# Decoder block on one core: three seven-product pairs, lower halves by an adding DMA, a rearranged tail

## The chip, the cores and the metric

The kernel runs on one core of a Trainium2 chip. The metric is device time in microseconds. TensorE multiplies, VectorE, ScalarE and GpSimd do element work, SyncE issues most DMAs.

## The reference

One post-norm decoder layer on 256 tokens of width 2048, in float32. It projects x to queries, keys, values and two gates, runs two causal attentions (a block-gated one, which for 256 tokens is plain causal attention, and a differential one), mixes them through two branch matrices and an output matrix, and normalizes. What the change touches is the second half:

```python
h = _layer_norm(DEEPNORM_ALPHA * h + mix, ln1_g[l], ln1_b[l])
g, u = jnp.split(h @ w_ffn_in, 2, axis=-1)          # 2048 -> 2 x 5632
ffn = (jax.nn.silu(g) * u) @ w_ffn_out              # 5632 -> 2048
h = _layer_norm(DEEPNORM_ALPHA * h + ffn, ln2_g[l], ln2_b[l])
```

## The kernel before

**Split products.** Every float32 product is three matmuls (`mm3`, lines 91 to 93). A weight tile is split into an upper half that ScalarE casts to fp32r (`split`, line 71) and a lower half, the rest, that VectorE subtracts (line 72). The activations are split the same way. A matmul takes a 128x128 stationary and a moving tile of 128x512.

**Feed-forward blocks.** The 256 rows are two row blocks (m = 0, 1). The first feed-forward matrix is worked in 11 column blocks of 512 gate and 512 up columns. Block 0 is done by two plain products (`product`). Blocks 1 to 10 go through `pair_product(j)`: eight pairs of K tiles, each with one 1 MB load by SyncE into a `raw` buffer of three (`load_pair`, line 716), and four accumulators in PSUM (gate and up, for each row block). The accumulator pool holds four, so the next block's first matmul needs one of this block's to be emptied.

An ordinary pair makes two upper and two lower halves 128x1024 wide (`halves`) and needs eight `mm3`, 24 matmuls. At the places in `SEVEN`, now pairs 4 and 6 of blocks 1 to 9, the 2x2 product of row blocks and K tiles is done with seven products instead of eight, 21 matmuls. VectorE then makes four combinations of the weights in place (lines 756 to 759), and ScalarE and VectorE split these too, as `t2` and `t3`. The activations' combinations are made once (`row_forms`). Three of the products gather in four PSUM tiles p1, p5, p6, p7 over the block's pairs of this kind; after the last one VectorE joins them (lines 771 to 774) and adds the accumulators at the block's end (lines 777 to 780). Then follow sigmoid, two multiplications and 32x32 transposes (line 264) for each row block.

**Buffers and order.** Upper and lower halves rotate through eight buffers each (`wh`, `wl`). The order of the instructions on each engine is laid out by the framework's planner from program order and its own durations, and is then fixed. `later(n, fn)` puts work n steps (`tick`) ahead in program order; a pair has two steps. `move_blocks` (line 286) is put eight steps ahead: 16 transfers of 32 KB within the chip, on SyncE's queue, which turn the transposed block into rows for the next product.

**Second matrix and tail.** The 44 K tiles of the second matrix are streamed once, and all eight accumulators of 128x512 (two row blocks, four column blocks) are held in PSUM. The last four K tiles (`TAIL`) are kept back for row block 1, so that row block 0 is done earlier: its residual, statistics and normalization (`norm`) run beside row block 1's remaining matmuls. `norm` has a fast form, two VectorE operations per piece, and a slow form, one ScalarE and two GpSimd operations. Row block 1's last column block is done in two halves of 256 columns; then residual, statistics, `norm` and stores follow.

Of the kernel before, what the change touches and what calls it, by code (L numbers as in the profile page):

```python
# [44 lines left out]
def decoder_block(ctx, tc, xT, x, wz, lam_qk, subln, wa, wb, wo, g1, b1, b1T, wf, wfp, wfo, g2, b2,  # L45
# [9 lines left out]
    def bigt(shape, dt, name):  # L55
        return big.tile([P] + shape, dt, tag="big", name=name)
# [4 lines left out]
    def small(name, n=4):  # L61
        return sm.tile([P, n], F32, tag="sm%d" % n, name=name)
# [487 lines left out]
    def cols(j):  # L550
        return slice(j * N, (j + 1) * N)
# [1 line left out]
    def quarters(*slow):  # L553
        return [(j * N, (j + 1) * N, j in slow) for j in range(4)]


    def norm(m, g, b, name, sink, pieces):
        mv = small("mv_" + name, 2)
        nc.vector.bn_aggr(mv, stats[m].rearrange("p a b -> p (a b)")[:, :6 * nstats[m]])
        rs = small("rs_" + name, 2)  # L560
        rsqrt_of(rs[:, 0:1], mv[:, 1:2], 1.0, LN_EPS)
        nc.vector.scalar_tensor_tensor(rs[:, 1:2], mv[:, 0:1], -1.0, rs[:, 0:1], op0=ALU.mult, op1=ALU.mult)
        for j, (c0, c1, slow) in enumerate(pieces):
            c = slice(c0, c1)
            h = hres[m][:, c]
            if not slow:
                nc.vector.scalar_tensor_tensor(h, h, mv[:, 0:1], g[:, c], op0=ALU.subtract, op1=ALU.mult)
                nc.vector.scalar_tensor_tensor(h, h, rs[:, 0:1], b[:, c], op0=ALU.mult, op1=ALU.add)
            else:
                nc.scalar.activation(h, h, AF.Identity, bias=rs[:, 1:2], scale=rs[:, 0:1])  # L570
                nc.gpsimd.tensor_mul(h, h, g[:, c])
                nc.gpsimd.tensor_add(h, h, b[:, c])
            sink(m, j, c, h)

    b1t = const.tile([P, KD], F32, name="b1t")
    nc.sync.dma_start(b1t, b1T)
    hth = [None] * NM
# [111 lines left out]

    SEVEN = (4, 6)
    forms = []

    def row_forms():
        ns = len(SEVEN)
        full = bigt([NM, 2 * ns, P], F32, "hfull")
        fs = bigt([4, ns, P], F32, "forms")
        hl = bigt([2, 4, ns, P], F32R, "formshl")
        for m in range(NM):  # L700
            for n, i in enumerate(SEVEN):
                nc.vector.tensor_add(full[:, m, 2 * n:2 * n + 2, :], hth[m][:, 2 * i:2 * i + 2, :], htl[m][:, 2 * i:2 * i + 2, :])
# [5 lines left out]
        split(fs, hl[:, 0], hl[:, 1])  # L708
        forms.append(hl)

    def stat_s(f, n):
        return forms[0][:, 0, f - 1, n, :], forms[0][:, 1, f - 1, n, :]

    def load_pair(j, i):
        raw = wp.tile([P, 4, N], F32, tag="raw", name="raw_fp%d_%d" % (j, i), bufs=3)
# [68 lines left out]
    for j in range(NB_F):  # L784
        if j % 2 == 0:

            act.append(bigt([2, 4, NM, 4, 32], F32, "act%d" % (j // 2)))
        rt = None
        ts_ = []

        def silu(m, gate):
            t = scr("sl%d_%d" % (j, m))
            nc.scalar.activation(t, gate, AF.Sigmoid)
            nc.vector.tensor_mul(t, t, gate)
            return t
# [12 lines left out]
        later(8, lambda j=j, rt=rt: move_blocks(act[j // 2][:, j % 2].rearrange("p i m h c -> p i (m h c)"),  # L808
                                                rt.rearrange("p b m n -> p b (m n)")))
# [12 lines left out]
    def sink2(m, j, c, h):  # L822
        nc.sync.dma_start(out[m * P:(m + 1) * P, c], h)

    def ffn_mm(m, kt, j, w, ac=None, c=slice(0, N)):
        ah, al, pairs = w
# [7 lines left out]

    HEAD = 2
    ahead = []
    for kt in range(KF):
        pairs = list(weights(wfo[kt * P:(kt + 1) * P, :], "fo%d" % kt))
        ahl = sp.tile([P, 2, S], F32R, tag="s", name="ahl%d" % kt)
        ah, al = ahl[:, 0, :], ahl[:, 1, :]  # L840
        part = act[kt // 8][:, kt % 8 // 4, :, :, kt % 4, :].rearrange("p i m c -> p m i c")
# [17 lines left out]
                ffn_mm(1, kt, j, w)  # L859
        else:  # L860
            done.append((kt, w))
    for j in range(NB_D):
        residual(0, cols(j), oacc[0, j])
    norm(0, lng2, lnb2, "ln2_0", sink2, quarters(2, 3))
    H = N // 2
    last = hres[1][:, cols(NB_D - 1)]
    nc.vector.scalar_tensor_tensor(last, last, ALPHA, oacc[1, NB_D - 1], op0=ALU.mult, op1=ALU.add)
    for j in range(NB_D - 1):
        for kt, w in done:
            ffn_mm(1, kt, j, w)  # L870
        residual(1, cols(j), oacc[1, j])
    j = NB_D - 1
    for i in range(2):
        rest = acc("rest%d" % i)[:, :H]
        for kt, w in done:
            ffn_mm(1, kt, j, w, rest, slice(i * H, (i + 1) * H))
        residual(1, slice(j * N + i * H, j * N + (i + 1) * H), rest, 1.0)
    norm(1, lng2, lnb2, "ln2_1", sink2, [(0, 512, False), (512, 896, True), (896, 1408, False), (1408, 1792, False),
                                         (1792, 2048, False)])


def _tables(half):
# [56 lines left out]
```

## Time and profile before

| | |
|---|---|
| runs, median (lowest, highest) | 1393.11 us (1388.95, 1393.82) |
| profiled execution, its own time | 1389.86 us |
| its span | 1388.1 us |
| TensorE busy | 1366.9 us (98%) |
| VectorE busy | 922.8 us (66%) |
| ScalarE busy | 638.0 us (46%) |
| GpSimd busy | 57.6 us (4%) |

The stages are limited by different things, so the shares of the whole span say little of one stage. Matmuls are pipelined: one shows 0.39 us, but the next starts before it ends. A gap of TensorE shows in the start times of a block's first matmul.

### The profile page before, as it was taken

The numbers are of one execution on the slowest core, as the hardware profiler recorded it, in microseconds if no ns is written. First come the engines' busy times: TensorE is split into PE (matmuls) and PEld (weight loads), VectorE is DVE, ScalarE is ACT, GpSimd is POOL, SyncE is SP. The second block draws the span as 40 slices with busy tenths as digits, with TensorE's granted clock in tenths as the row PEclk, the third lists the DMA queues.
The fourth block names the chain that finished last, engine by engine and source line by source line (L and its number), as shares of the span: only waits on it lengthen the run. The fifth ranks groups of instructions, "written<-read, shape, count | busy, mean of one in ns | idle before, by whom it ended". The sixth has DMA issues, their size and how long they took to land.

```text
span 1388.1 us, 16263 instructions
## 1 busy us (share of the span) xinstructions
PE 1366.9 (98%) x6104; PEld 1125.6 (81%) x6104; DVE 922.8 (66%) x1163; ACT 638.0 (46%) x859; POOL 57.6 (4%) x62
## 2 busy tenths in 40 slices
PE   9999999999999999999999999999999999999996
PEld 6788888888888888888888888787787888888885
DVE  6666566766545454575969887898778765545546
ACT  5363434546444434444634544445444455444440
POOL 1001010100000000100000000000000000000003
PEclk9999999999999999999999999999999999999998
DMA  8574645554464649573553654646646586555541
GB/s 291 182 299 145 235 153 196 196 198 152 159 240 145 246 157 369 189 263 120 176 179 139 244 223 175 232 158 243 223 170 230 193 310 244 187 193 201 184 150 61
DMA packets 57151, 279.45 MB, mean 201 GB/s; under 512 B 10224, under 2 KB 22640, under 8 KB 25712
## 3 DMA queue, kind: packets, MB, share of 16 engines
q1 hardware_dynamic: 57072, 278.41, 55.4%
q8 instruction: 48, 0.79, 0.2%
q14 instruction: 31, 0.25, 0.1%
HBM read 264.74 MB, written 2.10 MB: 192 GB/s over the span
## 4 chain that ended last, share of the span: by engine, by line
PE 83%; DVE 6%; DMA 6%; ACT 2%; issue 1%; SPq 0%; POOL 0%; ACTq 0%; DVEq 0%; POOLq 0%
PE oacc L93 5%; PE oacc L91 5%; PE oacc L92 5%; DMA raw_fp<-in_wfp 4%; PE acc_fg L91 4%; PE acc_fu L91 3%; PE acc_fg L93 3%; PE acc_fg L92 3%; PE acc_fu L93 3%; PE acc_fu L92 3%; PE acc_gA L91 2%; PE acc_gA L92 2%; PE acc_gB L92 2%; PE acc_gB L91 2%; PE acc_gB L93 2%; PE acc_gA L93 2%
## 5 line engine op out<-in xcount | busy, mean ns | idle before, releaser
L72 DVE TENSOR_TENSOR wl_fo<-raw_fo,wh_fo 128x1024 fp32r<-128x1024 f32 x88 | 107.3, 1224 | 106.5 <-ACT wh_fo L71 101.3
L71 ACT CAST wh_fo<-raw_fo 128x1024 fp32r<-128x1024 f32 x88 | 92.4, 1055 | 123.7 <-PE oacc L93 110.8
L93 PE MATMUL oacc<-wh_fo,ahl 128*128 128x512 f32 x348 | 135.5, 389 | 0.0
L92 PE MATMUL oacc<-wl_fo,ahl 128*128 128x512 f32 x348 | 135.4, 389 | 0.0
L91 PE MATMUL oacc<-wh_fo,ahl 128*128 128x512 f32 x348 | 135.4, 389 | 0.0
L93 PEld LDWEIGHTS oacc<-wh_fo,ahl 128*128 128x128 f32 x348 | 65.3, 188 | 13.8 <-DVE ahl L72 0.3
L92 PEld LDWEIGHTS oacc<-wl_fo,ahl 128*128 128x128 f32 x348 | 65.3, 188 | 13.7
L91 PEld LDWEIGHTS oacc<-wh_fo,ahl 128*128 128x128 f32 x348 | 65.3, 188 | 13.5
L72 DVE TENSOR_TENSOR wl_gA<-raw_gA,wh_gA 128x1024 fp32r<-128x1024 f32 x32 | 38.8, 1220 | 35.9 <-ACT wh_gA L71 35.9
L72 DVE TENSOR_TENSOR wl_o<-raw_o,wh_o 128x1024 fp32r<-128x1024 f32 x32 | 39.5, 1235 | 33.9 <-ACT wh_o L71 33.9
L71 ACT CAST wh_gA<-raw_gA 128x1024 fp32r<-128x1024 f32 x32 | 33.6, 1054 | 53.7 <-PE acc_brB L93 20.0
L71 ACT CAST wh_o<-raw_o 128x1024 fp32r<-128x1024 f32 x32 | 33.7, 1054 | 48.4 <-PE acc_o L93 33.5
L72 DVE TENSOR_TENSOR wl_gB<-raw_gB,wh_gB 128x1024 fp32r<-128x1024 f32 x32 | 38.6, 1222 | 19.6 <-ACT wh_gB L71 19.0
L91 PE MATMUL acc_o<-wh_o,mth 128*128 128x512 f32 x128 | 50.4, 394 | 0.0
L91 PE MATMUL acc_gA<-wh_gA,xth 128*128 128x512 f32 x128 | 50.2, 392 | 0.0
L91 PE MATMUL acc_gB<-wh_gB,xth 128*128 128x512 f32 x128 | 50.1, 391 | 0.0
L93 PE MATMUL acc_o<-wh_o,mtl 128*128 128x512 f32 x128 | 49.9, 390 | 0.0
L92 PE MATMUL acc_o<-wl_o,mth 128*128 128x512 f32 x128 | 49.8, 389 | 0.0
L93 PE MATMUL acc_gB<-wh_gB,xtl 128*128 128x512 f32 x128 | 49.8, 389 | 0.0
L92 PE MATMUL acc_gA<-wl_gA,xth 128*128 128x512 f32 x128 | 49.8, 389 | 0.0
L92 PE MATMUL acc_gB<-wl_gB,xth 128*128 128x512 f32 x128 | 49.8, 389 | 0.0
L93 PE MATMUL acc_gA<-wh_gA,xtl 128*128 128x512 f32 x128 | 49.8, 389 | 0.0
(498 smaller groups left out, 3723.8 us busy)
## 6 DMA issues: line engine op xcount, KB each, us to landing
raw_fp<-in_wfp SPq DMA_DIRECT2D x80, 1024.0 KB, 5.2
raw_fo<-in_wfo SPq DMA_DIRECT2D x44, 1024.0 KB, 4.8
raw_gA<-in_wz SPq DMA_DIRECT2D x16, 1024.0 KB, 4.8
raw_gB<-in_wz SPq DMA_DIRECT2D x16, 1024.0 KB, 5.0
raw_o<-in_wo SPq DMA_DIRECT2D x16, 1024.0 KB, 5.0
raw_vA<-in_wz SPq DMA_DIRECT2D x8, 1024.0 KB, 5.1
raw_qB<-in_wz SPq DMA_DIRECT2D x8, 1024.0 KB, 7.0
raw_kB<-in_wz SPq DMA_DIRECT2D x8, 1024.0 KB, 5.0
```

The lines of the kernel that those rows point to most:

```text
L71: nc.scalar.copy(hi, src)
L72: (eng or nc.vector).tensor_sub(lo, src, hi)
L91: nc.tensor.matmul(ac, xh, wh, start=start, stop=False)
L92: nc.tensor.matmul(ac, xh, wl, start=False, stop=False)
L93: nc.tensor.matmul(ac, xl, wh, start=False, stop=stop)
```

## The change

`SEVEN` becomes (1, 3, 5): three pairs of 21 matmuls in blocks 1 to 9. `row_forms` makes the combinations for three pairs, in two large buffers as before and two scratch tiles more, and is placed three steps into the product before block 1. In the pairs 0, 6 and 7 of each block (block 10 too), the lower half of the two up tiles is made without VectorE: ScalarE writes the negated cast into `wl`, casts into `wh`, and a DMA issued by GpSimd adds the raw tile to `wl`.

In the tail six K tiles are kept back; the splits of the first two of them lie in large buffers. The second normalization is written out in a fixed order. ScalarE copies most of g and b into PSUM tiles that have come free, and VectorE's fast form reads them there. Of row block 1 VectorE does columns 0 to 1408 and GpSimd two pieces of 320; before, it was one piece of 384. Two stores are issued from ScalarE's queue.

```diff
-    SEVEN = (4, 6)
+    SEVEN = (1, 3, 5)
...
-        hl = bigt([2, 4, ns, P], F32R, "formshl")
+        hl = bigt([2, 4, 2, P], F32R, "formshl")
+        more = [[sp.tile([P, 4, P], F32R, tag="s", name="forms%d_%d" % (n, k)) for k in range(2)] for n in range(2, ns)]
...
+    BY_DMA = (0, 6, 7)
+
+    def halves_by_dma(src, name):
+        wh = wp.tile([P, 2, N], F32R, tag="wh", name="wh" + name)
+        wl = wp.tile([P, 2, N], F32R, tag="wl", name="wl" + name)
+        nc.scalar.activation(wl, src, AF.Copy, scale=-1.0)
+        nc.scalar.copy(wh, src)
+        nc.gpsimd.dma_start(wl.bitcast(F32), src, accum_op=ALU.add)
+        return [(wh[:, a, :], wl[:, a, :]) for a in range(2)]
...
-                b22, b12 = halves(raw[:, 2:4], nm + "u")
+                b22, b12 = (halves_by_dma if i in BY_DMA else halves)(raw[:, 2:4], nm + "u")
...
+            later(3, row_forms)
             ups = product(wf[1], KD, stat_h, "fu0")
-            later(6, row_forms)
...
-    TAIL = 4
+    TAIL = 6
...
+    def waiting(src, name):
+        raw = wp.tile([P, 2048], F32, tag="raw", name="raw_" + name, bufs=3)
+        nc.sync.dma_start(raw, src)
+        for i in range(2):
+            both = bigt([4, N], F32R, "%s_%d" % (name, i))
+            split(raw[:, i * 1024:(i + 1) * 1024].rearrange("p (a n) -> p a n", n=N), both[:, 0:2, :], both[:, 2:4, :])
+            yield both[:, 0:2, :], both[:, 2:4, :]
...
+        load = waiting if KF - TAIL <= kt < KF - 4 else weights
+        pairs = list(load(wfo[kt * P:(kt + 1) * P, :], "fo%d" % kt))
...
+    def slow(m, c0, c1):
+        h = hres[m][:, c0:c1]
+        nc.scalar.activation(h, h, AF.Identity, bias=rs[m][:, 1:2], scale=rs[m][:, 0:1])
+        nc.gpsimd.tensor_mul(h, h, lng2[:, c0:c1])
+        nc.gpsimd.tensor_add(h, h, lnb2[:, c0:c1])
+
+    def fast(m, c0, c1, g, b):
+        h = hres[m][:, c0:c1]
+        nc.vector.scalar_tensor_tensor(h, h, rs[m][:, 2:3], g, op0=ALU.subtract, op1=ALU.mult)
+        nc.vector.scalar_tensor_tensor(h, h, rs[m][:, 0:1], b, op0=ALU.mult, op1=ALU.add)
...
+    share = [(0, N), (N, 2 * N), (2 * N, 2 * N + 384)]
...
+        nc.scalar.copy(gb[k, i], src[:, c0:c1])
...
+    with tc.manual_schedule():
+        for j in range(NB_D):
+            residual(0, cols(j), oacc[0, j])
...
+        moments(1)
+        shift(1)
+        ends = [(1408, 1728), (1728, 2048)]
+        for c in ends:
+            slow(1, *c)
+        for i, c in enumerate(share):
+            fast(1, *c, gb["g", i], gb["b", i])
+            put(nc.sync, 1, *c)
+        for c in ends:
+            put(nc.scalar, 1, *c)
```

## Rows read from the trace of the kernel before

**Rows 1.** The page: busy time by engine; shares of the chain of waits.
```profile
PE 1366.9 (98%) x6104; PEld 1125.6 (81%) x6104; DVE 922.8 (66%) x1163; ACT 638.0 (46%) x859; POOL 57.6 (4%) x62
...
PE 83%; DVE 6%; DMA 6%; ACT 2%; issue 1%; SPq 0%; POOL 0%; ACTq 0%; DVEq 0%; POOLq 0%
```

**Rows 2.** Windows: blocks 1 to 3, blocks 5 to 9, after the last matmul.
```profile
core 0: us, PE busy (x) PEld busy (x) DVE busy (x) ACT busy (x) POOL busy (x), PEclk, DMA share, GB/s
704.69:831.17 126.48, 126.48 (x559) 104.73 (x558) 101.30 (x118) 58.96 (x66) 0.00 (x0) 1.00 0.55 199
874.42:1091.19 216.77, 213.32 (x930) 173.76 (x931) 180.65 (x211) 101.57 (x115) 0.00 (x0) 1.00 0.56 205
1375.10:1388.10 13.00, 0.00 (x0) 0.00 (x0) 9.11 (x16) 0.71 (x1) 4.96 (x5) 0.66 0.34 125
```

**Rows 3.** Waits of 690 to 1100: who waited, for whom; total, times, longest.
```profile
DVE wlfp_5g L72 <- ACT whfp_5g L71: 36.2, 9, 4.9
...
DVE wlfp_4t L72 <- ACT whfp_4t L71: 10.8, 9, 1.2
DVE wlfp_6t L72 <- ACT whfp_6t L71: 10.7, 9, 1.2
...
PE acc_fg L91 <- DVE p L777: 3.6, 4, 1.2
```

**Rows 4.** Timeline of VectorE, one turn: start, duration, operation, idle before.
```profile
880.75 1.18 DVE L72 TENSOR_TENSOR wlfp_2g<-raw_fp,whfp_2g 128x1024 fp32r<-128x1024 f32 x1
...
882.99 1.22 DVE L72 TENSOR_TENSOR wlfp_3g<-raw_fp,whfp_3g 128x1024 fp32r<-128x1024 f32 x1
...
885.26 1.22 DVE L72 TENSOR_TENSOR wlfp_4g<-raw_fp,whfp_4g 128x1024 fp32r<-128x1024 f32 x1
...
891.17 2.36 DVE L72 TENSOR_TENSOR wlfp_4t<-raw_fp,whfp_4t 128x1024 fp32r<-128x1024 f32 x2 [1.19 <-ACT whfp_4t L71]
897.16 1.22 DVE L72 TENSOR_TENSOR wlfp_5g<-raw_fp,whfp_5g 128x1024 fp32r<-128x1024 f32 x1 [3.63 <-ACT whfp_5g L71]
...
923.58 1.19 DVE L72 TENSOR_TENSOR wlfp_2g<-raw_fp,whfp_2g 128x1024 fp32r<-128x1024 f32 x1
```

**Rows 5.** Timeline of SyncE's queue, the same turn.
```profile
880.85 10.01 SPq L286 DMA_DIRECT2D act<-rt  x16
890.98 27.47 SPq L716 DMA_DIRECT2D raw_fp<-in_wfp  x8
923.69 11.10 SPq L286 DMA_DIRECT2D act<-rt  x16
```

**Rows 6.** DMA issues: count, KB of each, median us to landing.
```profile
raw_fp<-in_wfp SPq DMA_DIRECT2D x80, 1024.0 KB, 5.2
...
act<-rt SPq DMA_DIRECT2D x176, 32.0 KB, 1.8
...
raw_qA<-in_wz SPq DMA_DIRECT2D x7, 512.0 KB, 5.6
```

**Rows 7.** Timeline of the tail, VectorE and GpSimd.
```profile
1367.51 0.26 DVE L559 BATCH_NORM_AGGREGATE mv_ln<-stats 128x2 f32<-128x24 f32 x1
...
1368.71 0.16 DVE L562 SCALAR_TENSOR_TENSOR rs_ln<-mv_ln,rs_ln 128x1 f32<-128x1 f32 x1 [0.39 <-POOL rs_ln L234]
...
1374.84 0.67 DVE L546 SCALAR_TENSOR_TENSOR hres<-hres,oacc 128x512 f32<-128x512 f32 x1
...
1376.93 0.40 DVE L546 SCALAR_TENSOR_TENSOR hres<-hres,rest 128x256 f32<-128x256 f32 x1
...
1377.83 0.29 DVE L559 BATCH_NORM_AGGREGATE mv_ln<-stats 128x2 f32<-128x30 f32 x1
...
1384.09 1.00 DVE L568 SCALAR_TENSOR_TENSOR hres<-hres,rs_ln,ln2b 128x384 f32<-128x384 f32 x2
...
1374.83 1.27 POOL L572 TENSOR_TENSOR hres<-hres,ln2b 128x512 f32<-128x512 f32 x1
...
1380.61 1.35 POOL L571 TENSOR_TENSOR hres<-hres,ln2g 128x384 f32<-128x384 f32 x1 [1.01 <-ACT hres L570]
```

More of the change, by code (lines that the diff above doesn't have):

```diff
@@ L554, in quarters @@
         return [(j * N, (j + 1) * N, j in slow) for j in range(4)]
[L557 to L573, printed above, removed]
     b1t = const.tile([P, KD], F32, name="b1t")
@@ L707, in row_forms @@
         nc.vector.tensor_sub(fs[:, 3], a[0][1], fs[:, 1])
-        split(fs, hl[:, 0], hl[:, 1])
-        forms.append(hl)
+        split(fs[:, :, 0:2], hl[:, 0], hl[:, 1])
+        for n in range(2):
+            forms.append([hl[:, k, :, n] for k in range(2)])
+        for n, hi_lo in enumerate(more):
+            split(fs[:, :, 2 + n], *hi_lo)
+            forms.append(hi_lo)
     def stat_s(f, n):
-        return forms[0][:, 0, f - 1, n, :], forms[0][:, 1, f - 1, n, :]
+        return tuple(t[:, f - 1, :] for t in forms[n])
     def load_pair(j, i):
@@ L818, in decoder_block @@
         oacc[0, j] = acc("oacc0_%d" % j)
-    TAIL = 4
+    TAIL = 6
     done = []
-    def sink2(m, j, c, h):
-        nc.sync.dma_start(out[m * P:(m + 1) * P, c], h)
     def ffn_mm(m, kt, j, w, ac=None, c=slice(0, N)):
@@ L836, in decoder_block @@
     ahead = []
+    def waiting(src, name):
[5 more added lines that the diff above has]
+            yield both[:, 0:2, :], both[:, 2:4, :]
     for kt in range(KF):
-        pairs = list(weights(wfo[kt * P:(kt + 1) * P, :], "fo%d" % kt))
+        load = waiting if KF - TAIL <= kt < KF - 4 else weights
+        pairs = list(load(wfo[kt * P:(kt + 1) * P, :], "fo%d" % kt))
         ahl = sp.tile([P, 2, S], F32R, tag="s", name="ahl%d" % kt)
@@ L861, in decoder_block, with moments @@
             done.append((kt, w))
-    for j in range(NB_D):
-        residual(0, cols(j), oacc[0, j])
-    norm(0, lng2, lnb2, "ln2_0", sink2, quarters(2, 3))
     H = N // 2
-    last = hres[1][:, cols(NB_D - 1)]
-    nc.vector.scalar_tensor_tensor(last, last, ALPHA, oacc[1, NB_D - 1], op0=ALU.mult, op1=ALU.add)
-    for j in range(NB_D - 1):
+    rs = [small("rs_ln2_%d" % m) for m in range(NM)]
+    def moments(m):
+        nc.vector.bn_aggr(rs[m][:, 2:4], stats[m].rearrange("p a b -> p (a b)")[:, :6 * nstats[m]])
+        rsqrt_of(rs[m][:, 0:1], rs[m][:, 3:4], 1.0, LN_EPS)
@@ new lines, in shift, with put @@
+    def shift(m):
+        nc.vector.scalar_tensor_tensor(rs[m][:, 1:2], rs[m][:, 2:3], -1.0, rs[m][:, 0:1], op0=ALU.mult, op1=ALU.mult)
+    def put(eng, m, c0, c1):
+        eng.dma_start(out[m * P:(m + 1) * P, c0:c1], hres[m][:, c0:c1])
+    def slow(m, c0, c1):
[7 more added lines that the diff above has]
+        nc.vector.scalar_tensor_tensor(h, h, rs[m][:, 0:1], b, op0=ALU.mult, op1=ALU.add)
@@ L869, in decoder_block, with copy, tail_mms @@
+    share = [(0, N), (N, 2 * N), (2 * N, 2 * N + 384)]
+    gb = {}
+    def copy(t, src, k, i):
+        c0, c1 = share[i]
+        gb[k, i] = t[:, :c1 - c0]
+        nc.scalar.copy(gb[k, i], src[:, c0:c1])
+    def tail_mms(j):
         for kt, w in done:
             ffn_mm(1, kt, j, w)
[L871 to L877, printed above, removed]
@@ L878, in decoder_block @@
-    norm(1, lng2, lnb2, "ln2_1", sink2, [(0, 512, False), (512, 896, True), (896, 1408, False), (1408, 1792, False),
-                                         (1792, 2048, False)])
+    with tc.manual_schedule():
+        for j in range(NB_D):
+            residual(0, cols(j), oacc[0, j])
+        last = hres[1][:, cols(NB_D - 1)]
+        nc.vector.scalar_tensor_tensor(last, last, ALPHA, oacc[1, NB_D - 1], op0=ALU.mult, op1=ALU.add)
+        moments(0)
+        copy(acc("g2_0"), lng2, "g", 0)
+        copy(acc("b2_0"), lnb2, "b", 0)
+        copy(tmp("g2_1"), lng2, "g", 1)
+        tail_mms(0)
+        shift(0)
+        slow(0, 2 * N, 3 * N)
+        slow(0, 3 * N, 4 * N)
+        for i in range(2):
+            fast(0, i * N, (i + 1) * N, gb["g", 0] if i == 0 else gb["g", 1],
+                 gb["b", 0] if i == 0 else lnb2[:, N:2 * N])
+            put(nc.sync, 0, i * N, (i + 1) * N)
+        residual(1, cols(0), oacc[1, 0])
+        copy(tmp("b2_1"), lnb2, "b", 1)
+        tail_mms(1)
+        residual(1, cols(1), oacc[1, 1])
+        copy(tmp("g2_2"), lng2, "g", 2)
+        for i in range(2, NB_D):
+            put(nc.sync, 0, i * N, (i + 1) * N)
+        tail_mms(2)
+        residual(1, cols(2), oacc[1, 2])
+        copy(tmp("b2_2"), lnb2, "b", 2)
+        j = NB_D - 1
+        for i in range(2):
+            rest = acc("rest%d" % i)[:, :H]
+            for kt, w in done:
+                ffn_mm(1, kt, j, w, rest, slice(i * H, (i + 1) * H))
+            residual(1, slice(j * N + i * H, j * N + (i + 1) * H), rest, 1.0)
+        moments(1)
[8 more added lines that the diff above has]
+            put(nc.scalar, 1, *c)
```

## Prediction

> **What bounds the kernel now.** I read the busy times and the chain of waits first, then the stretch of the feed-forward blocks in windows, the waits in it, one block's turn on VectorE and on SyncE's queue, and at last the tail. TensorE is busy for 98% of the span and holds 83% of the chain [rows 1]; a matmul count taken off it is time taken off, as long as its operands arrive. In the ten paired blocks (j = 1 to 10) they arrive only just. Blocks 1 to 3 take 126.48 us, 42.16 each [rows 2]. By the code each has six ordinary pairs of 24 matmuls and two of 21, 186 together, so a matmul costs 42.16 / 186 = 0.2267 us and nothing is lost there. Blocks 5 to 9 take 216.77, 43.35 each [rows 2], with the same 186: they lose 1.2 us apiece. The reader is to see where: the first matmul of a block waits for the VectorE addition that empties its accumulator (L777), 3.6 us in four visible waits [rows 3], so VectorE arrives late at the end of a block.
>
> VectorE is not late for lack of rate: it is busy 180.65 of 216.77 us, 36.1 a block [rows 2]. It is late because its queue is in order and has three gaps a block: 4.0 us before pair 5 (36.2 over nine), 1.2 before the second half of pair 4 and 1.2 before that of pair 6 (10.8 and 10.7 over nine) [rows 3]. The two short ones are ScalarE's cast, which can begin only when the last of four in-place subtractions is done. The long one goes back to SyncE: its queue issues 16 small transfers in 10.01 us from 880.85 and the weight loads of pairs 5 and 6 stand behind them; they go out from 890.98 [rows 5], take about 5.2 us to land [rows 6], and VectorE starts pair 5 at 897.16 after 3.63 us of nothing [rows 4]. One turn, from pair 2 to the next block's pair 2, is 880.75 to 923.58, 42.83 us [rows 4], against 42.16 of TensorE. So the late blocks are VectorE's turn, and TensorE waits for it.
>
> **The matmuls removed.** One more pair of 21 in nine blocks: 27 matmuls, 6.1 us. TensorE's own block becomes 183 x 0.2267 = 41.48, so nine blocks need 373.3 where they take 1091.19 - 704.69 = 386.5 now. That is the ceiling, -13.2 us, if no operand is ever late. The last block, j = 10, has no such pair and stays.
>
> **What the third pair costs VectorE.** An ordinary pair occupies it from 880.75 to 882.99, 2.24 us. A seven-product pair starts at 885.26; its last double split starts at 891.17 and ends at 893.53: 8.27 us, 1.19 of it waiting [rows 4]. Turning one into the other adds 6.03. ScalarE gets two casts more, 1.8 us at its mean of 0.88 (101.57 / 115); it is idle for half of the block [rows 2], which covers them.
>
> **What the adding DMA gives back.** Three lower halves leave VectorE in each block. Half an ordinary pair is 1.12 us, so 3.4. ScalarE does one more cast for each, 2.6 us a block by the same mean; behind them stand the casts of pairs 7, 0 and 1 on its queue, which its idle half covers too. Thirty DMAs are issued by GpSimd, idle in this stretch. No row shows an adding DMA. The nearest from below is a 32 KB transfer inside the chip, 1.8 us; from above a load of equal size, 512 KB, 5.6 us [rows 6]. I take 4, nearer the equal size. It replaces a VectorE split of 1.22, so these halves come about 3 us later after their cast, and the raw buffer (one of three) is held as much longer before the next load may start. Pair 6's upper half needs it first: TensorE has six matmuls, 1.4 us, between the pair's start and the need. With loads behind it as late as now, this eats the lead and no more; at 5.6 it can stop TensorE by up to 2 us a block. By the Trainium skill, page DMA: Bandwidth & Descriptors, section Anatomy of one DMA, a transfer from GpSimd's queue costs about 2.0 us plus its bytes at 436 GB/s; the estimate from that is 3.2 us for 512 KB. It would make the lateness 2 us instead of 3 and leave the sum as it is.
>
> **The places.** With the three pairs at i = 1, 3, 5, the four additions that join the products (L771 to L774) run before pair 6, no longer in the last pair. That clears L777, the addition for which TensorE waits now. But pair 1's 8.27 us move into the same stretch.
>
> **The new turn.** Between the small transfers and pair 5 lie pairs 2, 3 and 4: two ordinary and one of seven products, before and after alike. So pair 5's load is as late as now, and its gap stays. Nothing in the change touches the 16 transfers or their place behind pair 4's load. The turn then is 43.35 + 6.03 - 3.4 = 46.0 us. If the order laid out by the planner fills one of the three cast gaps (it does put a split of pair 1 between the joining additions now, but fills neither cast gap), it is 44.8; I take that. It exceeds 41.48, so VectorE sets the block. At the start there is some lead (three blocks lost nothing), now used up in the first block: 41.5 + 8 x 44.8 = 399.9, against 386.5: **+13.4 us**. From below, with all gaps covered, it is -13.2; from above, with 46.0 from block 2 on, 41.5 + 368 = 409.5, +23.
>
> **The operand forms** are made some ten pair steps earlier, in the product before block 1, and are half as many again: three operations more on VectorE, wider ones besides, about 3 us at its mean of 0.86 (180.65 / 211) [rows 2], and a cast on ScalarE. The lead that let blocks 1 to 3 lose nothing covers them; without it, it is 3 us, once. Behind them on VectorE stand the lower halves of that product and of block 1's first pairs. Two more scratch tiles stay occupied; the six that are left are what one block uses.
>
> **The tail.** Now TensorE ends at 1375.10 and 13.00 us follow [rows 2]. VectorE reaches the last residual only at 1376.93 [rows 7], 1.8 us after its operand, because the first row block's normalization is still in its queue. Six K tiles kept back give 24 more matmuls, 5.4 us, to cover it, so the residual starts some 0.1 after TensorE. Then: residual to aggregate 0.9 (1376.93 to 1377.83); aggregate to the shift 1.2, as for the first row block (1367.51 to 1368.71), because no two-operand work of VectorE runs beside GpSimd's two small steps; 1.0 through the shift and ScalarE's first columns to GpSimd (1.01 idle now, for 384 columns); four GpSimd steps of 320. Such a step is between 1.27 x 320/512 = 0.8, the one beside a VectorE operation with its operand in PSUM, and 1.35 x 320/384 = 1.1 [rows 7]: 3.2 to 4.5. Last, 3.0 from the last result to the end (1385.09 to 1388.10). Sum 9.4 to 10.7; VectorE's side is 0.1 + 0.9 + 1.2 + 0.2 + 3.8 + 3.0 = 9.2, with 0.67 for 512 columns beside GpSimd [rows 7]. I take 10.0: **-3.0 us**. The six copies of g and b are ScalarE's, idle there; on the queue of ScalarE only the two last stores stand behind its work. The two K tiles in large buffers cost what the others cost; twelve more narrow matmuls add 0.1.
>
> The Trainium skill, page SBUF — State Buffer, section Who interferes with whom, says that a VectorE instruction with two SBUF inputs contends with a GpSimd instruction that reads SBUF, and the second to start blocks. Taken fully, a PSUM operand frees GpSimd and the steps are 0.8, a tail of 9.4; the trace's fastest step agrees, and the sum would move by 0.6.
>
> **Sum.** On the profiled execution of 1389.86 (span 1388.1, 1.8 around it): + 13.4 - 3.0 = 1400.3. The median of the runs, 1393.11, is 3.3 above that execution and their lowest, 1388.95, 0.9 below; halfway to the median gives **1402**. The likeliest case's own range is 1395 to 1411.
>
> **Rivals.**
> - *VectorE's gaps close* (the other side). The planner lays out the order anew, and a gap lasts only if nothing ready is queued in it. If pair 5's load gets ahead of the small transfers, or other work fills the 4.0 us, the turn is 42.0 and the nine blocks 41.5 + 8 x 42.0 = 377.5; with the cast gaps filled too, 373.3. With the tail: 1378 to 1374, some 1377 to 1381 as a median. It decides at a turn of 43.0. For it: L771 to L774 come earlier and VectorE's work without gaps, 37.0 (43.35 less 6.4 of gaps) + 4.8 - 3.4 = 38.4, is below 41.48. Against: those gaps were there in all nine blocks. Chance 0.36.
> - *It evens out*: half the long gap goes and a turn is 43.4: 41.5 + 347.2 = 388.7, +2.2 - 3.0, so 1389 to 1393. Chance 0.16.
> - *The adding DMA is the bound*: if it takes longer than a load of its size, both TensorE's wait for pair 6 and the next block's load after it grow, 3 us a block more: 1425. For it: three raw buffers, DMA engines busy 0.56 of the time already [rows 2]. Against: GpSimd is free, and the reads stay on the chip. Chance 0.10.
> - The forecast has 0.38.
>
> 0.5% is about what a measurement of this kernel can tell from no change, 7 us. Faster is the first rival, 0.36; same the second, 0.16; slower the rest, 0.48. The range 1375 to 1416 leaves out most of the third rival and the lower edge of the first.
>
> **What would show it.** Right: blocks 2 to 9 of 44 to 46 us, VectorE idle before pair 5 for about 4 us behind SyncE's 16 transfers, TensorE waiting inside seven-product pairs instead of at the block's first matmul, the tail near 10 us. Wrong: blocks of 41.5 (gaps closed), or TensorE's waits ending on the adding DMA.

## The result, and the profile after

The changed kernel takes **1442.45 us** (median of four, 1441.62 to 1443.09) where the kernel before, beside it, takes 1392.34: a ratio of 1.0365, 95% interval 1.0347 to 1.0382. It is slower by 50 us. The sign of the forecast holds; its size, 1402, and its range, up to 1416, do not.

The busy times of the page, which answer to [rows 1]: TensorE shows 21 matmuls fewer and more busy time, a first sign that matmuls ran slower or stood in line. (Line numbers are each kernel's own: in the changed kernel the in-place steps are L753 to L756, the joins L768 to L771 and the additions at a block's end L774 to L777.)
```profile
PE 1389.5 (96%) x6083; PEld 1125.5 (78%) x6083; DVE 928.3 (64%) x1188; ACT 681.8 (47%) x915; POOL 83.6 (6%) x94
```
Windows of the changed kernel, cut at the first matmul of a block: block 1, blocks 2 to 5, block 6, blocks 7 to 9, and what follows the last matmul. The columns are those of [rows 2].
```profile
704.37:750.29 45.92, 43.40 (x184) 35.42 (x183) 29.76 (x37) 21.44 (x24) 2.58 (x3) 0.96 0.67 209
750.29:947.38 197.09, 179.43 (x733) 138.28 (x732) 148.78 (x181) 99.36 (x114) 10.42 (x12) 0.97 0.67 210
947.38:994.35 46.97, 43.68 (x185) 33.65 (x183) 37.48 (x46) 22.97 (x27) 2.61 (x3) 1.00 0.64 206
994.35:1141.77 147.42, 135.54 (x550) 104.67 (x549) 112.31 (x136) 74.35 (x85) 7.83 (x9) 0.97 0.71 225
1431.12:1441.30 10.18, 0.00 (x0) 0.00 (x0) 5.25 (x10) 1.20 (x2) 4.14 (x6) 0.62 0.27 103
```
Nine blocks take 1141.77 - 704.37 = 437.4 us, 48.6 each, where they took 386.5 [rows 2]: +50.9. From block 10's first matmul to the last one it is 289.35 for 283.91 before, +5.4: pair 0's addition stops TensorE for 2.0 us there too, and the first products of the second matrix wait 1.1. The tail is 10.18 us for 13.00. With 0.3 us gained ahead of block 1 that makes the 53.2 us between the two profiled spans (1441.3 and 1388.1). GpSimd, the fifth busy time, now has three instructions a block: the issues of the adding DMAs. The granted clock is 0.96 to 0.97 in most blocks and 1.00 in block 6, which is also the second shortest.

The waits of the changed kernel from 690 to 1150 (who waited, for whom; total, times, longest), which answer to [rows 3]:
```profile
DVE p L774 <- PE acc_fg L93: 37.8, 8, 6.0
...
PE acc_fu L92 <- DMA wlfp_6u<-raw_fp: 18.4, 9, 2.7
...
PE acc_fu L92 <- DMA wlfp_0u<-raw_fp: 8.1, 7, 2.9
...
PE p L91 <- ACT whfp_1t L71: 6.8, 13, 1.2
```
TensorE stops at the adding DMA of pair 6 in all nine blocks and at that of pair 0 in most. And VectorE, which the forecast had as the bound, now waits for TensorE, 37.8 us: its addition of the first product (L774) cannot begin before the stopped matmuls are done.

The DMA issues of the changed kernel (count, KB of each, median us to landing), for [rows 6]:
```profile
wlfp_0u<-raw_fp POOLq DMA_DIRECT2D x10, 512.0 KB, 9.9
wlfp_6u<-raw_fp POOLq DMA_DIRECT2D x10, 512.0 KB, 5.3
wlfp_7u<-raw_fp POOLq DMA_DIRECT2D x10, 512.0 KB, 4.9
```
One stop, in the timelines of ScalarE, GpSimd and TensorE (start, duration, operation, idle before):
```profile
927.28 2.00 ACT L71 CAST whfp_5t<-raw_fp 128x1024 fp32r<-128x1024 f32 x2 [5.10 <-DVE raw_fp L756]
...
930.61 1.04 ACT L719 CAST whfp_6u<-raw_fp 128x1024 fp32r<-128x1024 f32 x1
931.55 1.06 ACT L718 ACTIVATE wlfp_6u<-raw_fp 128x1024 fp32r<-128x1024 f32 x1
```
```profile
932.91 0.87 POOL L720 DMA_DIRECT2D wlfp_6u<-raw_fp  x1 [41.51 <-ACT wlfp_6u L718]
```
```profile
935.97 0.39 PE L93 MATMUL acc_fg<-whfp_7g,htl 128*128 128x512 f32 x1
939.02 0.80 PE L92 MATMUL acc_fu<-wlfp_6u,hth 128*128 128x512 f32 x1 [2.65 <-DMA wlfp_6u<-raw_fp]
939.61 0.63 PE L93 MATMUL acc_fu<-whfp_6u,htl 128*128 128x512 f32 x1
...
942.13 0.40 PE L91 MATMUL acc_fu<-whfp_6u,hth 128*128 128x512 f32 x1
```
ScalarE works through its queue in order. It sits idle for 5.10 us until VectorE has done pair 5's in-place subtractions, casts pair 5's t halves, and only then pair 6. The addition is asked for at 932.91, TensorE is there at 936.36 (935.97 + 0.39) although the planner has already drawn matmuls of pairs 6 and 7 ahead, and the sum lands at 939.0: 6.1 us to landing against a lead of 3.4. After the stop the matmuls follow each other at about 0.43 us instead of 0.2267, seven steps in 3.11 us for 1.59: another 1.5 us. The clock in windows of 2 us goes with it: it falls to 0.50, the 1.2 GHz level, after the stop.
```profile
934.00:936.00 2.00, 2.00 (x10) 1.31 (x8) 1.58 (x2) 1.45 (x2) 0.25 (x1) 1.00 1.02 295
936.00:938.00 2.00, 0.37 (x2) 0.00 (x0) 0.25 (x1) 1.33 (x2) 0.62 (x1) 1.00 1.08 213
...
940.00:942.00 2.00, 2.00 (x6) 1.57 (x5) 0.00 (x0) 0.00 (x0) 0.79 (x1) 0.50 0.99 260
942.00:944.00 2.00, 2.00 (x10) 1.60 (x10) 0.28 (x1) 0.00 (x0) 0.00 (x0) 0.98 0.99 311
```

### The profile page after: what moved, and what is told of

It reads as the page before. It is cut to its first block, busy times and chain, and to the rows that moved or that the text cites. A ratio compares the mean times of both kernels' runs of the same rounds, so it can differ in the third digit from the quotient of the medians.

```text
span 1441.3 us, 16463 instructions
## 1 busy us (share of the span) xinstructions
PE 1389.5 (96%) x6083; PEld 1125.5 (78%) x6083; DVE 928.3 (64%) x1188; ACT 681.8 (47%) x915; POOL 83.6 (6%) x94
## 5 line engine op out<-in xcount | busy, mean ns | idle before, releaser
L72 DVE TENSOR_TENSOR wl_fo<-raw_fo,wh_fo 128x1024 fp32r<-128x1024 f32 x84 | 102.1, 1224 | 99.7 <-ACT wh_fo L71 95.1
L71 ACT CAST wh_fo<-raw_fo 128x1024 fp32r<-128x1024 f32 x84 | 87.7, 1054 | 115.3 <-PE oacc L93 95.0
L91 PE MATMUL oacc<-wh_fo,ahl 128*128 128x512 f32 x332 | 129.6, 390 | 1.2 <-DVE sl L791 0.9
L92 PE MATMUL oacc<-wl_fo,ahl 128*128 128x512 f32 x332 | 129.2, 389 | 0.0
L93 PE MATMUL oacc<-wh_fo,ahl 128*128 128x512 f32 x332 | 128.7, 389 | 0.0
L91 PEld LDWEIGHTS oacc<-wh_fo,ahl 128*128 128x128 f32 x332 | 62.3, 188 | 15.6 <-ACT ahl L71 1.3
L93 PEld LDWEIGHTS oacc<-wh_fo,ahl 128*128 128x128 f32 x332 | 62.3, 188 | 13.1
L92 PEld LDWEIGHTS oacc<-wl_fo,ahl 128*128 128x128 f32 x332 | 62.3, 188 | 12.6
L91 PE MATMUL acc_gB<-wh_gB,xth 128*128 128x512 f32 x128 | 50.1, 391 | 0.0
```

The lines of the kernel that those rows point to most:

```text
L71: nc.scalar.copy(hi, src)
L72: (eng or nc.vector).tensor_sub(lo, src, hi)
L91: nc.tensor.matmul(ac, xh, wh, start=start, stop=False)
L92: nc.tensor.matmul(ac, xh, wl, start=False, stop=False)
L93: nc.tensor.matmul(ac, xl, wh, start=False, stop=stop)
```

## Experiments

"Theory L" below is that an adding DMA costs what its landing overruns the lead that its cast has on TensorE; "theory H" that it costs by itself, by traffic and by the raw buffer that it holds. Each kernel was timed beside the kernel before (1389.9 to 1390.8 us). Pairs are counted from 0; three of the expectations below count them from 1 and say 1, 7 and 8 for the pairs 0, 6 and 7.

**The tail alone**: two pairs at 4 and 6 as before, the new tail.

> The kernel before with the new tail alone (two pairs of seven products and every lower half on VectorE, as before). The tail after the last matmul was 13.0 us before and is 10.2 us in the changed kernel's trace, and nothing ahead of it is touched but one K tile pair that is kept back: every theory expects 1389 to 1390 us, a ratio of 0.998, with some 10.2 us from TensorE's last matmul to the end. A time at 1392 or above would say that keeping six K tiles back costs earlier what the tail saves.

Measured 1388.79, ratio 0.9984 (0.9975 to 0.9993): -1.7 us, as expected.

**All lower halves by VectorE.**
```diff
-    BY_DMA = (0, 6, 7)
+    BY_DMA = ()
```


> The changed kernel with all lower halves made by VectorE's subtraction: three pairs of seven, new tail, no adding DMA. Theory A (the adding DMAs make TensorE wait and hold the raw buffers, and everything else of the change is small): the blocks fall from 48.6 us to 43 to 45 and the time to 1385 to 1405 us, depending on how much of VectorE's 40.8 us a block then shows. Theory B (the recorded forecast: VectorE's turn with SyncE's sixteen transfers sets the block, and the three lower halves taken from it are a relief): taking them back adds 3.4 us a block, so 1442 + 9 x 3.4 = 1473 us. Theory C (the three pairs themselves, by the order of matmuls that they force, cost the 51 us): about 1442 us.

Measured 1408.45, ratio 1.0127 (1.0114 to 1.0141). Nearest to theory A, 3 us above its range; B and C fall: without the adding DMA the kernel is 34 us faster. But three pairs of seven still cost 20 us against two. Block 1 takes 41.97 us, blocks 2 to 9 take 365.16 / 8 = 45.6 each:
```profile
705.24:747.21 41.97, 41.65 (x185) 34.20 (x183) 33.98 (x41) 18.21 (x21) 0.00 (x0) 1.00 0.58 213
747.21:1112.37 365.16, 346.38 (x1465) 278.01 (x1465) 322.85 (x382) 175.90 (x202) 0.00 (x0) 0.98 0.55 197
```
VectorE's timeline and TensorE's first late matmul in this kernel:
```profile
929.67 0.69 DVE L776 TENSOR_TENSOR u<-u,acc_fg 128x512 f32<-128x512 f32 x1 [0.30 <-PE acc_fg L93]
...
938.66 0.69 DVE L756 TENSOR_TENSOR raw_fp<-raw_fp 128x512 f32<-128x512 f32 x1
940.54 2.36 DVE L72 TENSOR_TENSOR wlfp_1t<-raw_fp,whfp_1t 128x1024 fp32r<-128x1024 f32 x2 [1.19 <-ACT whfp_1t L71]
```
```profile
940.56 0.50 PE L91 MATMUL p<-whfp_1t,formshl 128*128 128x512 f32 x1 [2.09 <-ACT whfp_1t L71]
```
From the block's last additions to pair 1's last in-place subtraction VectorE works 9.7 us without a gap (929.67 to 938.66 + 0.69), then ScalarE casts; TensorE has pair 0 and nine matmuls of pair 1 in between, 33 x 0.2267 = 7.5 us, and stops for 2.09.

**The addition left out**: the lower halves of pairs 0, 6 and 7 stay minus the rounded halves.
```diff
-        nc.gpsimd.dma_start(wl.bitcast(F32), src, accum_op=ALU.add)
```


> The changed kernel with the adding DMA left out: both casts stay on ScalarE, but the lower halves of pairs 1, 7 and 8 are minus the rounded halves and not the differences. Theory A (adding DMA): every wait on it is gone and VectorE keeps its relief, so blocks of 41.8 to 43 us, 9 x (48.6 - 42.5) = 55 us less and 1380 to 1392 us. Theory B (VectorE's turn of 44.8 us with SyncE's transfers): 1400 to 1408 us. Theory C (order of the matmuls of three pairs): near 1442 us.

Measured 1404.1, ratio 1.0111 (1.009 to 1.0131). This is theory B's number, 1400 to 1408: the kernel that the forecast described, one whose adding DMA costs nothing, takes what the forecast said. What it left out is the DMA's 37 us. Block 1 takes 42.45 us, blocks 2 to 9 take 358.01 / 8 = 44.8 each, and TensorE still waits for pair 1's t halves (window and wait of this kernel):
```profile
747.35:1105.36 358.01, 344.13 (x1464) 272.64 (x1465) 297.02 (x359) 199.29 (x226) 0.00 (x0) 1.00 0.55 202
```
```profile
PE p L91 <- ACT whfp_1t L71: 9.2, 14, 1.6
```

**A copy in place of the addition.**
```diff
-        nc.gpsimd.dma_start(wl.bitcast(F32), src, accum_op=ALU.add)
+        nc.gpsimd.dma_start(wl.bitcast(F32), src)
```


> The changed kernel with the same DMA on the same queue as a plain copy from the raw weights into the lower half, without the addition, so the lower halves of pairs 1, 7 and 8 hold the whole weights. It separates the adding from the transfer. If the addition itself makes the transfer long (4.9 to 9.9 us to landing for 512 KB in the changed kernel's trace), the copy lands in 3 to 5 us and the time falls by a half of the 51 us or more, to 1400 to 1420 us. If it is the place in the order (ScalarE's late cast, GpSimd's issue, the raw buffers that are held until the DMA has read them), the copy lands in about the same 5 to 10 us and the time stays at 1435 to 1445 us.

Measured 1422.48, ratio 1.0228 (1.0214 to 1.0243), between the two expectations. The DMA issues of this kernel:
```profile
wlfp_0u<-raw_fp POOLq DMA_DIRECT2D x10, 512.0 KB, 7.8
wlfp_6u<-raw_fp POOLq DMA_DIRECT2D x10, 512.0 KB, 4.1
wlfp_7u<-raw_fp POOLq DMA_DIRECT2D x10, 512.0 KB, 3.0
```
A copy lands 1.2 to 2.1 us sooner than an addition, and the kernel is 18 to 20 us faster. It still costs 18 over none.

**A copy that nothing reads**, to a scratch area in HBM.
```diff
-        nc.gpsimd.dma_start(wl.bitcast(F32), src, accum_op=ALU.add)
+        nc.gpsimd.dma_start(dr.tile([P, 2, N], F32, tag=name, name="dr" + name), src)
```


> The changed kernel with the three DMAs a block sent as plain copies of the raw weights to a scratch area in HBM that nothing reads; the lower halves are the minus casts and not the differences, so no engine waits for a DMA from GpSimd's queue, while the traffic (512 KB each) and the hold on the raw buffers stay. Without any such DMA it took 1404.1 us, with the copy into the lower half 1422.5 us. Theory L (TensorE's wait for the landing is what costs): 1402 to 1408 us. Theory H (traffic and held raw buffers): 1415 to 1425 us.

Measured 1409.67, ratio 1.0135 (1.0115 to 1.0154): between the two theories, nearer L. These copies land as late as those that are read (7.7, 4.4 and 3.0 us in the median). Of the 18 us that a copy costs over none, traffic and held buffers are then some 6, TensorE's wait and what follows from it 12. The other 18 us, by which an addition costs more than a copy, this run doesn't part: an addition lands later, so it is both waited for and holds its buffer longer.

**One adding DMA, at pair 6, and the other two, at 0 and 7.**

> The changed kernel with the adding DMA at the pair numbered 6 alone; pairs 0 and 7 get VectorE's subtraction again. No adding DMA is 1408.5 us, three are 1442.5 us. Theory L (what counts is how late the addition is asked for: ScalarE casts pair 6 only after pair 5's t halves, and TensorE stands 22.6 us at the lower half of pair 6 but 7.3 us at that of pair 0): this one carries most of the 34 us, 1428 to 1438 us. Theory H (each addition costs alike, by the raw buffer that it holds and by its transfer among the loads): a third, 1417 to 1423 us.

> The other part: adding DMAs at the pairs numbered 0 and 7, VectorE's subtraction at pair 6. Theory L: 1412 to 1420 us, since TensorE's waits on these two are a third of those on pair 6. Theory H: two thirds of the 34 us, 1428 to 1434 us.

Measured 1438.77 (ratio 1.0356, 1.0326 to 1.0386) and 1432.94 (1.0305, 1.0286 to 1.0323). The first is theory L's number but for 0.8 us, the second theory H's, and the two don't add up: 30 and 24 us over 1408.5 where both together cost 34. With pair 6's addition gone the stop moves to pair 7's (19.4 us of TensorE's waits in place of 18.4). One late addition a block is nearly enough for the whole loss.

**Pair 6 cast early**, all three additions.
```diff
+            if i == 5:
+                nxt = load_pair(j, 6)
+                up = halves_by_dma(nxt[:, 2:4], "fp%d_6u" % j)
+                ready[6] = halves(nxt[:, 0:2], "fp%d_6g" % j), up
             t2, t4 = halves(raw[:, 0:2], nm + "t2")
```


> The changed kernel, all three adding DMAs, but ScalarE makes pair 6's minus cast and its rounded halves before it takes up pair 5's t halves, for which it now waits 5.1 us idle. The addition for pair 6 is then asked for some 5 to 7 us sooner, all else as in the changed kernel. Theory L: TensorE's stop at the lower half of pair 6 (2.7 us a block, 2.6 us more until its clock is back) goes, 9 x 2.5 to 9 x 3.5, so 1411 to 1420 us. Theory H: the addition still takes as long and holds its buffer as long: 1435 to 1445 us.

Measured 1442.41, ratio 1.0375 (1.036 to 1.0391): no gain; the number is theory H's. GpSimd's and TensorE's timelines of this kernel:
```profile
921.60 0.87 POOL L720 DMA_DIRECT2D wlfp_6u<-raw_fp  x1 [34.95 <-DVE raw_fp L759]
928.74 0.87 POOL L720 DMA_DIRECT2D wlfp_7u<-raw_fp  x1 [6.26 <-DVE wlfp_7g L72]
```
```profile
937.80 0.80 PE L92 MATMUL acc_fu<-wlfp_7u,hth 128*128 128x512 f32 x1 [4.03 <-DMA wlfp_7u<-raw_fp]
```
Pair 6's addition, asked for early, makes nobody wait. Pair 7's is now the late one: asked for at 928.74 it lands 9.0 us later, and TensorE stops for 4.03. So the run doesn't decide between the theories.

**Pair 6 cast early, and it alone by adding DMA**: the same edit with BY_DMA = (6,).

> One adding DMA a block, at the pair numbered 6, with that pair's casts made before pair 5's t halves; pairs 0 and 7 by VectorE's subtraction. The same single DMA with the casts in the changed kernel's order took 1438.8 us, no adding DMA 1408.5 us. Theory L (landing against lead): asked for 5 to 11 us sooner, the addition lands before TensorE comes to it (in the run with three, 4.4 us to landing, 926.0 against a first use at 928.4), and nothing behind it waits for a DMA, so 1402 to 1412 us. Theory H (an adding DMA costs by itself at this place, or its wait only moves on to pair 7, as it did with three of them): 1430 to 1440 us.

Measured 1408.3, ratio 1.0127 (1.0111 to 1.0144). The single addition that cost 30 us costs nothing once its cast goes ahead. It still takes 4.7 us to land in the median, for 5.4 (who waited for the tile, us and times; its landing times):
```profile
  PE acc_fu L92: 0.5, 1
...
DMA to landing us min/median/max: 4.4/4.7/7.4
```
SyncE's loads still wait for it, 80.9 us in nine blocks for 65.4 in the late one. For pair 6, then, the price is landing against lead, theory L. Two things stay open: the new order without any adding DMA was not run, and the sum hides two changes against the kernel with all subtractions, nine blocks of 399.6 us for 407.1, and 290.6 for 283.5 from there to the last matmul.

**One adding DMA where casts run ahead**: the kernel of the tail alone with BY_DMA = (1,).

> The kernel before with the new tail, two pairs of seven at 4 and 6, and one adding DMA a block, at the pair numbered 1, which is cast while VectorE and TensorE are a pair or more ahead. Without the adding DMA it takes 1388.8 us. Theory L (an adding DMA costs what its landing overruns the lead that the cast has on TensorE): the lead here is 6 us or more against 4.9 to 9.9 us to landing, so 1388 to 1400 us. Theory H (each adding DMA costs by itself, by traffic and the held raw buffer, as the single one at pair 6 did, 30 us): 1410 to 1420 us.

Measured 1389.06, ratio 0.999 (0.9979 to 1.0002): nothing, as theory L has it. GpSimd's issue and TensorE's first use of the half:
```profile
915.71 0.86 POOL L720 DMA_DIRECT2D wlfp_1u<-raw_fp  x1 [41.76 <-PE acc_fg L93]
```
```profile
924.21 0.39 PE L92 MATMUL acc_fu<-wlfp_1u,hth 128*128 128x512 f32 x1
```
8.5 us of lead, against a landing of 5.2 in the median (8.5 at most).

**Two pairs of seven, adding DMAs at 0 and 1; and at 0 alone.**

> The version that the runs point to: two pairs of seven at 4 and 6 as before, new tail, and adding DMAs only where their casts run ahead of TensorE, at the pairs numbered 0 and 1. Theory L: no wait on a DMA, VectorE relieved of 2.3 us a block which it does not need, so 1386 to 1390 us, at or just under the 1388.8 us of the tail alone. If the addition of pair 0, cast some 8 us ahead, lands late when two are in the queue together, 1393 to 1410 us.

> The kernel before with the new tail and one adding DMA a block, at the pair numbered 0. The same at the pair numbered 1 took 1389.1 us, at both 1445.4 us, and there SyncE's loads waited 84.5 us for pair 0's addition and ScalarE 54.0 us for pair 3's load, while TensorE waited for no DMA. If pair 0's addition alone holds up the loads (it lands in 9.1 us, the buffer is the one for pair 3), 1420 to 1445 us. If it takes two of them in one queue, 1387 to 1395 us.

Measured 1445.4 (1.0402, 1.0379 to 1.0426), above both expected ranges, and 1440.94 (1.0359, 1.034 to 1.0379), the first outcome. A second price, which theory L does not have. The timelines of ScalarE and VectorE with the addition at pair 0 alone:
```profile
948.90 1.05 ACT L71 CAST whfp_3g<-raw_fp 128x1024 fp32r<-128x1024 f32 x1 [4.47 <-DMA raw_fp<-in_wfp]
949.86 0.62 ACT L790 ACTIVATE sl<-u 128x512 f32<-128x512 f32 x1
```
```profile
950.51 0.69 DVE L791 TENSOR_TENSOR sl<-sl,u 128x512 f32<-128x512 f32 x1 [4.76 <-ACT sl L790]
```
Its waits on SyncE's queue:
```profile
SPq L702 <- DMA wlfp_0u<-raw_fp: 83.7, 9, 11.3
```
The load of pair 3 needs pair 0's raw buffer and so waits for the addition, 9.0 us to landing in the median. Pair 3's cast stands ahead of the second sigmoid of the block before on ScalarE's queue; VectorE waits for the sigmoid, with all of pairs 2 to 4 behind. TensorE's own wait on that DMA is 5.5 us in seven times; it waits more for VectorE, 12.2 for pair 2's lower half and 11.7 at a block's first matmul. The held buffer alone is not the price. With the addition at pair 1 SyncE waits as long (87.4 us in ten), and ScalarE sits idle before pair 4's cast; but there both sigmoids stand ahead of that cast:
```profile
918.92 0.63 ACT L790 ACTIVATE sl<-u 128x512 f32<-128x512 f32 x1
...
925.24 1.05 ACT L71 CAST whfp_4g<-raw_fp 128x1024 fp32r<-128x1024 f32 x1 [4.74 <-DMA raw_fp<-in_wfp]
```

**The same two as unread copies.**

> Two pairs of seven at 4 and 6, new tail, the DMAs at the pairs numbered 0 and 1 sent as plain copies to a scratch area in HBM that nothing reads; these lower halves are minus casts and not differences. With additions into the lower halves it took 1445.4 us. If the held raw buffers and the traffic make the 56 us, they remain with the copies, somewhat shorter: 1415 to 1440 us. If it is a wait for the sums that the profile puts down to other engines, 1386 to 1392 us.

Measured 1399.49, ratio 1.0068 (1.0046 to 1.0089): neither. Pair 0's copy lands in 2.9 us for 9.1, so its buffer is held a third as long, and 11 of the 57 us over the tail alone remain. Hold and landing aren't parted cleanly by this run; that the load of pair 3 is what comes late is read from the waits.

**GpSimd subtracts.**
```diff
-        nc.scalar.activation(wl, src, AF.Copy, scale=-1.0)
         nc.scalar.copy(wh, src)
-        nc.gpsimd.dma_start(wl.bitcast(F32), src, accum_op=ALU.add)
+        nc.gpsimd.tensor_sub(wl, src, wh)
```


> The changed kernel with the three lower halves of a block (pairs 1, 7 and 8) made by a subtraction on GpSimd, from the raw weights and the rounded half, in place of ScalarE's minus cast and the adding DMA. The copy in place of the addition left 1422.5 us and no DMA at all 1404.1 us. If what costs is the DMA (its way through the queue and its landing) and VectorE's relief is worth the 4.4 us between 1408.5 and 1404.1, then GpSimd, idle for 94% of the span, gives 1400 to 1408 us, as long as one subtraction of 128x1024 takes 3 to 4 us (its 128x320 steps take 0.87 us in the tail, which makes 2.8 us for 1024). If GpSimd's subtraction takes over 5 us or makes VectorE's steps longer while it runs (1.22 us for a subtraction now), TensorE waits again: 1415 to 1435 us.

Measured 1414.81, ratio 1.0176 (1.0161 to 1.0191): the lower edge of the second outcome. The groups of GpSimd and VectorE in this kernel (busy, mean ns | idle):
```profile
L719 POOL TENSOR_TENSOR wlfp_7u<-raw_fp,whfp_7u 128x1024 fp32r<-128x1024 f32 x10 | 33.1, 3306 | 1.6 <-ACT whfp_7u L718 1.6
```
```profile
L72 DVE TENSOR_TENSOR wlfp_7g<-raw_fp,whfp_7g 128x1024 fp32r<-128x1024 f32 x10 | 26.0, 2603 | 3.2 <-ACT whfp_7g L71 3.2
```
GpSimd's step takes 3.3 us, and the subtraction that VectorE runs beside it 2.60 instead of 1.22. The relief is more than given back: the kernel is 6 us slower than with all subtractions on VectorE.

**Three pairs at 2, 4 and 6, without and with one adding DMA.**
```diff
-    SEVEN = (1, 3, 5)
-    BY_DMA = (0, 6, 7)
+    SEVEN = (2, 4, 6)
+    BY_DMA = ()
```


> Three pairs of seven at the pairs numbered 2, 4 and 6 in place of 1, 3 and 5, every lower half by VectorE's subtraction, new tail. With 1, 3 and 5 it took 1408.5 us, and TensorE stood 18.1 us in nine blocks at the t halves of pair 1, which VectorE prepares right behind the end of the block before (joins, additions, sigmoid products, transposes). Theory P (place: that wait comes from the nearness to the block's end): it goes, and 1388 to 1397 us remain. Theory V (VectorE's 40.8 us of work in a turn of 41.5 us of matmuls is too much wherever the pairs stand): the wait moves to another pair, 1404 to 1412 us.

> Both together: pairs of seven at 2, 4 and 6, one adding DMA a block at the pair numbered 1, new tail. Against the same without the adding DMA: VectorE has 1.1 us a block less to do. Theory L: as that kernel or up to 10 us less if VectorE bounds it, 1383 to 1405 us. Theory H: 20 to 30 us more than that kernel.

Measured 1426.6 (1.0253, 1.0236 to 1.027) and 1428.87 (1.0275, 1.0255 to 1.0295). Theory P falls, and V's number is too low: TensorE now waits for pair 0's lower half (VectorE, 17.4 us), which stands behind pair 6's joins and the block's last steps. The adding DMA at pair 1 adds 2.3 us to that, where theory H had 20 to 30.

**Two pairs at 3 and 5.**
```diff
-    SEVEN = (1, 3, 5)
-    BY_DMA = (0, 6, 7)
+    SEVEN = (3, 5)
+    BY_DMA = ()
```


> Two pairs of seven at the pairs numbered 3 and 5 in place of 4 and 6, no adding DMA, new tail, the operand forms made before the first block's second product as in the changed kernel. If the third pair costs by VectorE's time (34.8 us of work in a turn with two pairs, 40.8 us with three), two at 3 and 5 take 1386 to 1393 us. If the place costs (nearer to the block's start, so VectorE's joins and t halves meet other work), 1397 us or more.

Measured **1379.78**, ratio 0.9924 (0.9907 to 0.994): below the lower expected range, faster than the kernel before by 10 us and than any other here. Blocks 2 to 9 of this kernel, then of the kernel of the tail alone:
```profile
747.05:1084.33 337.28, 337.28 (x1489) 279.28 (x1488) 288.39 (x336) 166.46 (x183) 0.00 (x0) 1.00 0.57 213
```
```profile
746.50:1092.84 346.34, 341.07 (x1489) 278.09 (x1488) 286.62 (x334) 162.93 (x183) 0.00 (x0) 1.00 0.56 206
```
TensorE never stops and VectorE has 288.39 of 337.28 to do. A block turns in 42.2 us, where it takes 43.3 with the tail alone; VectorE's work is the same, and its joins run a pair earlier than with 4 and 6. The operand forms are also made earlier here than in that kernel. Both kernels begin block 2 at about 747 and the gain grows over the eight blocks after it, which speaks for the places; no run parts the two.

The ladder, each against the kernel before beside it: tail -1.7; third pair, in these places +19.7 (to +18.0); VectorE's relief -4.4 (+13.6); traffic and held buffers +5.9 (+19.5); waiting for a landing of copies +12.5 (+32.0); adding instead of copying +18.1 (+50.1). The four runs with the addition left out spread over 9 us, so the steps of 4.4 and 5.9 are known to some 4 us only.

## Why the prediction was wrong, point by point

- **The step that failed** is the adding DMA's term: "I take 4 ... this eats the lead and no more", which put nothing into the sum. It is +36.5 us (50.1 - 13.6), 4.1 a block. The size was off a little at pair 6 (5.3) and far at pair 0 (9.9; up to 11.4): the load of 512 KB, taken as the row from above, was no upper bound. The lead was not what the forecast had either, because pair 6 is cast behind pair 5's t halves. And the sum had VectorE's turn as the block, with no term for a stop of TensorE beside it. A stop of TensorE near the block's end holds back VectorE's additions (L774 waits 37.8 us); VectorE then starts pair 1 later, and TensorE waits there again, 6.8 us in thirteen times, where it waits 9.2 with the addition left out. So the new stops, 18.4 + 8.1 us, come for the most part on top of the old ones. The matmuls at half rate come on top of that: read from the starts of all matmuls between 700 and 1190, steps of 0.40 to 0.50 us lose 11.2 us over 0.2267 each, with the addition left out 1.0. All of TensorE's waits between 690 and 1150 come to 37.3 us, 14.5 with the addition left out; with the slow steps that is 33.0 of the 36.9 us by which the nine blocks differ (437.4 and 400.5).
- **Its rival** had this mechanism, with 3 us a block, 1425 and a chance of 0.10. Its place, TensorE's wait for pair 6, was right, its price a quarter short of 4.1; the chance was too small. Its other half, a later load in the next block, is not what costs by the waits: ScalarE's first cast of pair 1 waits for its load 13.4 us in seven blocks, and 16.0 in eight without any adding DMA. The bound of 5.6 was given as able to stop TensorE by 2 us a block, and that was left out of the sum although 5.6 was the row of equal size. TensorE's wait at pair 6 is just that, 18.4 / 9 = 2.0 us a block.
- **VectorE's turn** was 44.8 by the forecast from block 2 on, and is 44.8 with the addition left out: right in size, by luck, with two errors that cancel. The forecast kept pair 5's gap, and it did not stay: VectorE starts pair 5 after 0.25 us of nothing (in [rows 4] 3.63), though SyncE's 16 transfers still stand before the loads. Changed kernel, SyncE and VectorE:
```profile
951.85 10.01 SPq L286 DMA_DIRECT2D act<-rt  x16
961.97 36.64 SPq L702 DMA_DIRECT2D raw_fp<-in_wfp  x8
```
```profile
958.77 1.22 DVE L72 TENSOR_TENSOR wlfp_2g<-raw_fp,whfp_2g 128x1024 fp32r<-128x1024 f32 x1
...
971.84 1.23 DVE L72 TENSOR_TENSOR wlfp_5g<-raw_fp,whfp_5g 128x1024 fp32r<-128x1024 f32 x1 [0.25 <-ACT whfp_5g L71]
```
  In the kernel before, the transfers begin as VectorE begins pair 2 (880.85 and 880.75); here they begin 6.9 us ahead of it, because pair 1's longer work now lies between. With the addition left out the gap is nearly gone too: 8.9 us in five blocks, for 36.2 in nine. So the first rival was right about that gap: with all subtractions on VectorE the turn is 45.6, where the forecast's rows give 43.35 + 6.03 = 49.4. But closing it did not bring the turn to 41.5, because pair 1's steps follow the block's end and TensorE waits for them. The three cast gaps stayed, 1.2 each; the forecast had one of them filled.
- **The relief** of 3.4 us a block on VectorE took 0.9 off the turn (45.6 to 44.8); VectorE waits for casts and matmuls instead.
- **The 27 matmuls** are gone, but no block of the changed kernel reaches 41.5; block 1 takes 45.92. The lead that was to carry block 1 is there: it takes 41.97 with all subtractions on VectorE and 42.45 with the addition left out. The adding DMAs' stops use it up.
- **The operand forms**, made early for two pairs, cost nothing that two pairs at 3 and 5 show: TensorE is busy in all of their blocks. What they cost for three pairs no run parts.
- **The tail** is right: 10.0 foreseen, 10.18 measured. Of its 2.8 us the time shows 1.7 by itself, with an interval that holds the 2.8 (1.0 to 3.5).

## What to carry to other kernels

Work taken off a busy engine and given to a DMA has two prices: its landing against the lead that the request has, where an in-order queue can make the request late, and the buffer that it holds until then, which delays the load three pairs on and costs where another engine's work is queued behind that load's cast. Before sizing either, look which engine waits for which at the end of the turn: where two nearly full engines feed each other, a stop of one isn't hidden by the other's being the bound. Here the place of the extra work in the turn was worth much: two pairs at 3 and 5 take 9 us less than at 4 and 6, and a third pair, in the two places tried, loses 20 or more.

## What the runs showed of the hardware

- An adding DMA of 512 KB inside the chip lands in 4.4 us at best and in 11.8 at most, with medians of 4.7 to 9.9 by kernel and place; a copy of the same lands 1.2 to 2.1 us sooner in the median, and GpSimd's issue of the addition takes 0.87 us. The estimate of 3.2 us that the Trainium skill gave (page DMA: Bandwidth & Descriptors, section Anatomy of one DMA) is near the two faster copies in the medians above, 3.0 and 4.1, and far from the third, 7.8; no addition here was that short.
- After the stop shown above, 2.65 us, TensorE's granted clock falls to 0.50 and is back some 3 us later; after the stop of 2.09 us with all subtractions on VectorE it stays at 1.00, as after those of up to 1.2 us of the kernel before [rows 2, 3].
- Beside a two-operand subtraction on GpSimd, VectorE's takes 2.60 us for 1.22, with tiles of 128x1024. By the Trainium skill, page SBUF — State Buffer, section Who interferes with whom, such two contend, and the second to start blocks; the trace agrees: one of VectorE's starts 1.2 us after GpSimd's and ends 1.1 after it (923.63 to 926.45 beside 922.44 to 925.37).
